# One decoder layer on one core: VectorE in program order at three handovers, a seven-tile start of the mixer, and half of the embedding projection moved

## The chip, the core and the metric

The kernel runs on one core of a Trainium2 chip. Five engines run their own instruction streams: TensorE (PE; its weight loads are shown as PEld), VectorE (DVE), ScalarE (ACT), GpSimd (POOL) and SyncE (SP), which here only starts transfers. The metric is the device time of one execution in microseconds, as the median of several runs.

## What is computed

One step of a decoder layer for 256 prompt columns and 8 sample columns, 264 columns in all:

```python
h = h + 0.5 * rmsnorm(swiglu(rmsnorm(h, ..), w_ffn1_gate, w_ffn1_up, w_ffn1_down), ..)
mix, cb, xb, hs = token_mixer(rmsnorm(h, norm_mix_pre), ...)
h = h + rmsnorm(mix, norm_mix_post)
h = h + 0.5 * rmsnorm(swiglu(rmsnorm(h, ..), w_ffn2_gate, w_ffn2_up, w_ffn2_down), ..)
gate = sigmoid(rmsnorm(h, norm_ple_pre) @ w_ple_gate)
h = h + rmsnorm(gate * (p @ w_ple_proj), norm_ple_post)

# token_mixer(u)
glu_a, glu_b, z, xbc, dt_raw = split(u @ w_in)
v   = silu(layernorm(causal_dwconv31(glu_a * sigmoid(glu_b))))
x, B, C = split(silu(causal_dwconv4(xbc)))       # 3072, 8*128, 8*128
y   = ssd(x, softplus(dt_raw + dt_bias), -exp(a_log), B, C, d_skip, h0)   # 8 groups
yg  = groupwise_rmsnorm(y * silu(z)) * ssm_norm_g
out = concat(v, yg) @ w_out
```

The model width is 2048 (16 tiles of 128 rows, numbered k), the FFN width 5632 (44 tiles). The new states of both convolutions and of the scan are outputs too.

## The kernel before

**Layout and matmuls.** Features lie on the partitions, the 264 columns on the free axis. Each product of a 128x128 weight tile with 128x264 activations is three matmuls (`mm3`, L248 to L252): high part of the weight with the high and the low part of the activation, then the low part of the weight with the high part. So every activation is split in two (`split`, L254: a conversion on ScalarE at L258 or L243, a remainder on VectorE at L216 or L219), and so is every weight.

**Weights.** `PLAN` lists units of up to 16 weight tiles in the order of use. `Weights` (L128 to L165) loads each unit in two halves of up to 8 tiles: a transfer into `wraw` by SyncE, a conversion `whi` on ScalarE (L154), a remainder `wlo` on VectorE (L155). Each has four buffers, two units' worth, and the loading runs two units ahead (`AHEAD`).

**Stages, in order.** FFN 1; *handover 1*; the input projection of the mixer with convolutions, scan and gates between; the output projection; *handover 2*; FFN 2; *handover 3*; the gate projection and the end. At a handover the sum of a norm over all 16 tiles must be complete before the first tile of the next stage can be scaled, and the next stage opens *wide* (`gemm_first`): it runs over k in the outer loop and feeds several output tiles at once, so that it can start with one activation tile. The FFNs and the gate projection open with 7 output tiles (`FIRST_FF`, `FIRST_PG`), the mixer with 4 (dt, B0, C0, x0), in 4 units of 4 k. All other output tiles are computed one by one (`gemm_one`). The accumulators: a pool `acc` of five PSUM banks, a pool `ps` of three. With four tiles open one bank of `acc` is still free; with seven, all five and two of `ps` are taken.

**Handover 1.** `rs` is the scale of the FFN's result, `r` that of the mixer's input; r comes from the same sums by a chain of products (`q2`). The residual is updated for each k by `tt(t, ys[k], rs)` and `tt(H(k), H(k), t)`, and u is `H(k)` times r times a gain. Updates of k above 0 are added on GpSimd, some of the products too. The projection of the per-layer embedding (`pproj`, 96 matmuls in two units `pp`, which depend on nothing in the layer) fills TensorE's time in this gap. The residual is then stored to DRAM (`hsave`).

**The mixer.** `IN_ORDER` lists the output tiles. For each of the 8 groups: B, C, three x, three z, with pairs of GLU tiles (ga, gb) put between at `GLU_IN`. The taps of the long GLU convolution are queued and done a few at a time on VectorE. `do_dt` makes dt, its decays and their sums, with a trip through DRAM to spread them over partitions. `decays` (L696) loads the sums and makes the decay matrices on ScalarE; `ssd` is the scan of a group, with transposes of x on TensorE (L727) and state products (L753). `gate` (L809) multiplies y by Silu(z), squares on ScalarE, adds twice on GpSimd (`SumSq`, tile `run`, L216), sums over partitions by a matmul with ones on TensorE (`total`, L306), and scales. It is called one group late, at x0 of the next group.

**Order.** A list scheduler orders each engine's instructions by its own reckoning of when they are ready, with program order as priority; the engines then run in that order. `high_priority` lifts some. `after` (L243) keeps the activation tables of ScalarE (Silu, Sigmoid, Ln and Exp) in program order, since a change of table is an instruction of its own (L238).

## Time and profile before

| | us |
|---|---|
| median of 3 runs | 2435.34 |
| the runs | 2430.39, 2435.34, 2436.11 |
| profiled execution | 2432.44 |
| its span in the profile | 2430.7 |
| TensorE busy | 2367.7 (97%) |
| VectorE busy | 1569.2 (65%) |
| ScalarE busy | 1181.4 (49%) |
| GpSimd busy | 298.4 (12%) |

The mean granted clock of TensorE is 0.993. A row of the profile's groups names line, engine, operation, output and inputs, then count, busy time, the mean of one in ns, and after a bar the idle time of the engine just before, with what ended it. `PE ps L306 <- POOL run L216` in the list of waits is a matmul of line 306 that waited for a GpSimd operation of line 216 on the tile `run`. A row of a timeline begins with the start time and the duration; rows of the same kind are put together (`x4`), and in brackets stands how long the engine was idle before, and what it waited for. Matmuls are pipelined, so a matmul of 0.28 us in a timeline may be followed by the next after 0.12.

### The profile page before, as it was taken

To read this page: it belongs to the slowest core of one execution; us is meant where nothing else is said; L and a number is where in the kernel's file an instruction comes from. 1 tells how busy PE (TensorE), PEld (TensorE's weight loads), DVE (VectorE), ACT (ScalarE), POOL (GpSimd) and SP (SyncE) were. 2 spreads that over 40 slices of the span, in tenths; PEclk is the share of its full clock that TensorE was granted. 3 is DMA by queue.
4 is the path that set the end of the run, shared out by engine and by line. 5 is a ranking of instruction groups with operands and counts; after the bars stand their busy time and mean duration, and the time that the engine had idled before them with its cause. 6 is when DMAs were issued, how large, how long until landed. Compare 5 with 4: busy or idle time off the path is not lost.

```text
span 2430.7 us, 47409 instructions
## 1 busy us (share of the span) xinstructions
PE 2367.7 (97%) x19448; PEld 2342.7 (96%) x19448; DVE 1569.2 (65%) x2333; ACT 1181.4 (49%) x1771; POOL 298.4 (12%) x295
## 2 busy tenths in 40 slices
PE   8999999999999889999999999999999999999988
PEld 8999999999999889999999999999999999999988
DVE  6554455545557858988798975766545565565585
ACT  6444444433456465665565545544444443344465
POOL 0400000000015212122122010101000000000103
PEclk9999999999999999999999999999999999999999
DMA  7655555555556666666666556476766776676553
GB/s 249 217 183 184 182 183 182 183 183 183 183 169 207 213 180 193 207 216 202 210 216 205 181 181 216 153 238 228 240 213 223 237 236 217 217 236 206 184 191 132
DMA packets 166250, 489.89 MB, mean 202 GB/s; under 512 B 25568, under 2 KB 42640, under 8 KB 166032
## 3 DMA queue, kind: packets, MB, share of 16 engines
q1 hardware_dynamic: 166032, 486.86, 62.0%
q8 instruction: 152, 2.49, 0.4%
q14 instruction: 66, 0.54, 0.1%
HBM read 465.65 MB, written 22.42 MB: 201 GB/s over the span
## 4 chain that ended last, share of the span: by engine, by line
PE 84%; DVE 6%; issue 3%; ACT 3%; DMA 2%; POOL 1%; SPq 0%; ACTq 0%; POOLq 0%; DVEq 0%
PE acc L250 27%; PE acc L251 27%; PE acc L252 27%; DVE wlo L155 2%; DVE y L219 1%; ACT whi L154 1%; PE ps L306 1%; DVE h L216 1%; DMA ab<-d_cs 1%; DMA cbc<-d_bc 1%; DVE ych L794 1%; PE ps L250 0%; ACT tmp L243 0%; DMA d_bc<-rows 0%; PE ps L251 0%
## 5 line engine op out<-in xcount | busy, mean ns | idle before, releaser
L252 PE MATMUL acc<-act,wlo 128*128 128x264 f32 x6224 | 1770.7, 285 | 4.3 <-DVE wlo L155 4.1
L251 PE MATMUL acc<-act,whi 128*128 128x264 f32 x6224 | 1756.6, 283 | 6.3 <-DVE act L216 6.2
L250 PE MATMUL acc<-act,whi 128*128 128x264 f32 x6224 | 1747.7, 283 | 3.4 <-DVE tmp L216 2.1
L155 DVE TENSOR_TENSOR wlo<-wraw,whi 128x1024 fp32r<-128x1024 f32 (+2 forms) x812 | 986.9, 1217 | 597.9 <-ACT whi L154 595.5
L154 ACT CAST whi<-wraw 128x1024 fp32r<-128x1024 f32 (+2 forms) x812 | 829.9, 1026 | 961.9 <-PE acc L251 717.3
L250 PEld LDWEIGHTS acc<-act,whi 128*128 128x128 f32 x6224 | 1175.5, 190 | 6.0 <-issue 2.1
L251 PEld LDWEIGHTS acc<-act,whi 128*128 128x128 f32 x6224 | 1169.2, 188 | 9.9 <-DVE act L216 7.9
L252 PEld LDWEIGHTS acc<-act,wlo 128*128 128x128 f32 x6224 | 1167.9, 188 | 8.3 <-DVE wlo L155 6.4
L216 POOL TENSOR_TENSOR run<-run,tmp 128x264 f32<-128x264 f32 x93 | 87.8, 944 | 962.9 <-ACT tmp L243 961.8
L216 POOL TENSOR_TENSOR s<-s,eap 128x1024 f32<-128x1024 f32 x24 | 48.8, 2035 | 630.4 <-DMA s<-in_hst 630.4
L219 DVE SCALAR_TENSOR_TENSOR y<-v,vec,y 128x251 f32<-128x251 f32 (+23 forms) x240 | 118.1, 512 | 1.2
L219 DVE SCALAR_TENSOR_TENSOR s<-bb,xds,s 128x128 f32<-128x128 f32 x192 | 52.7, 346 | 66.1 <-POOL s L216 66.1
L216 POOL TENSOR_TENSOR h<-h,cbc 128x512 f32<-128x512 f32 x48 | 73.6, 1553 | 166.0 <-DMA cbc<-d_bc 90.9
L258 ACT CAST act<-tmp 128x264 fp32r<-128x264 f32 x120 | 48.7, 410 | 69.9 <-DVE tmp L216 55.2
L216 DVE TENSOR_TENSOR tmp<-acc,rr 128x264 f32<-128x264 f32 x100 | 43.0, 430 | 51.0 <-PE acc L252 50.8
L216 DVE TENSOR_TENSOR tmp<-tmp,acc 128x264 f32<-128x264 f32 x86 | 36.7, 427 | 38.7 <-PE acc L252 38.6
L216 DVE TENSOR_TENSOR act<-tmp,act 128x264 fp32r<-128x264 f32 x120 | 56.1, 471 | 0.3
L243 ACT ACTIVATE tmp<-tmp 128x264 f32<-128x264 f32 x112 | 47.0, 420 | 8.7 <-DVE tmp L216 8.4
L243 ACT ACTIVATE tmp<-y 128x264 f32<-128x264 f32 x67 | 28.0, 425 | 44.1 <-DVE y L216 43.0
L216 DVE TENSOR_TENSOR y<-y,acc 128x264 f32<-128x264 f32 x80 | 34.0, 425 | 24.0 <-PE acc L252 24.0
L794 DVE TENSOR_REDUCE ych<-h 128x4 f32<-128x512 f32 x48 | 32.4, 678 | 17.5 <-POOL h L216 17.5
L250 PE MATMUL ps<-act,whi 128*128 128x264 f32 x96 | 28.4, 304 | 15.4 <-ACT whi L154 8.1
(165 smaller groups left out, 926.1 us busy)
## 6 DMA issues: line engine op xcount, KB each, us to landing
wraw<-in_w SPq DMA_DIRECT2D x756, 512.0 KB, 4.7
h<-in_hst SPq DMA_DIRECT2D x48, 256.0 KB, 3.9
s<-in_hst SPq DMA_DIRECT2D x24, 512.0 KB, 6.5
out_nss<-s SPq DMA_DIRECT2D x24, 512.0 KB, 3.0
wraw<-in_w SPq DMA_DIRECT2D x24, 384.0 KB, 4.1
wraw<-in_w SPq DMA_DIRECT2D x32, 256.0 KB, 3.9
ab<-d_cs SPq DMA_DIRECT2D x16, 384.0 KB, 5.1
cbc<-d_bc SPq DMA_DIRECT2D x8, 512.0 KB, 4.3
```

The source lines that it names most:

```text
L154: nc.scalar.copy(hi, raw)
L155: nc.vector.tensor_tensor(out=lo, in0=raw, in1=hi.bitcast(F32), op=ALU.subtract)
L216: return (eng or nc.vector).tensor_tensor(out=out, in0=in0, in1=in1, op=op)
L219: return nc.vector.scalar_tensor_tensor(out=out, in0=in0, scalar=scalar, in1=in1, op0=op0, op1=op1)
L243: i = nc.scalar.activation(out=out, in_=in_, func=func, bias=bias, scale=scale)
L250: nc.tensor.matmul(acc, hi, x[:, 0, :], start=first, stop=False)
L251: nc.tensor.matmul(acc, hi, x[:, 1, :], start=False, stop=False)
L252: return nc.tensor.matmul(acc, lo, x[:, 0, :], start=False, stop=last).ins
L258: nc.scalar.copy(t[:, 0, :], x)
L306: nc.tensor.matmul(p, ones, s, start=i == 0, stop=i == len(self.parts) - 1)
L794: nc.vector.tensor_reduce(out=ych[:, j, b : b + 4], in_=h0, op=ALU.add, axis=AX.X)
```

## The change

1. **VectorE in program order at the handovers** (`in_order`, `handed`): from the handover until the wide start is issued, VectorE's instructions stand as the program writes them. The program is written so that they interleave: `update_h(0..3)` between the steps of q2, then `make_u(k)` (scale, split, update of k + 4) two per unit of the wide start, through `feed`; `Weights.fill` puts the loads behind them. At handovers 2 and 3 the class `Update` does the same (five steps ahead, then two per unit).
2. **No GpSimd at handover 1**: 15 additions and 7 products go to VectorE.
3. **The mixer opens seven tiles wide** (`FIRST_IN`), in 8 units of 2 k. For group 0 the three z tiles come ahead of C: dt, B0, z0, z1, z2, C0, x0. Then x1, x2, B1 and so on one by one.
4. **`GLU_IN`** has three pairs amid the mixer instead of four; the other five follow at the end.
5. **The second half of the embedding projection** (48 matmuls) moves to handover 3.
6. **Decays**: the sample decay is exponentiated before its trip through DRAM (`ed`) rather than behind it; `load_sums` starts the loads at C, `decays` only computes. For group 0 the scan is put off until B1 has come (`early`).
7. **Gates** in two: `gate_begin` at C of the next group, `gate_end` where `gate` stood, its total no earlier than the last matmul written before it (`traced`).
8. `btm` has two buffers; the stores of the residual come behind the wide start.

What it moves on VectorE at handover 1. Before, from the first product of r's chain (`tmp_9007` is q2, `rr_9000` is rs, `rr_9018` is r, `h_85` holds the residual of the first four k):

```order
492 L216 TENSOR_TENSOR tmp_9007<-ps_9008,rr_9000 128x264
493 L216 TENSOR_TENSOR tmp_9190<-y_2456,rr_9000 128x264
494 L216 TENSOR_TENSOR tmp_9193<-y_2519,rr_9000 128x264
495 L216 TENSOR_TENSOR tmp_9196<-y_2582,rr_9000 128x264
496 L219 SCALAR_TENSOR_TENSOR tmp_9007<-ps_9012,tmp_9007 128x264
497 L216 TENSOR_TENSOR h_85<-h_85,tmp_9190 128x264
498 L216 TENSOR_TENSOR tmp_9007<-tmp_9007,rr_9000 128x264
499 L219 SCALAR_TENSOR_TENSOR tmp_9007<-rr_295,tmp_9007 128x264
500 L155 TENSOR_TENSOR wlo_0_9024<-wraw_0_9022,whi_0_9023 128x1024
501 L155 TENSOR_TENSOR wlo_8_9030<-wraw_8_9028,whi_8_9029 128x1024
502 L219 SCALAR_TENSOR_TENSOR tmp_9199<-h_85,vec,rr_9018 128x264
```

The same place after (q2 is `tmp_9010`, rs `rr_9003`, r `rr_9033`):

```order
494 L226 TENSOR_TENSOR h_85<-h_85,tmp_9015 128x264
495 L229 SCALAR_TENSOR_TENSOR tmp_9010<-ps_9018,tmp_9010 128x264
496 L226 TENSOR_TENSOR tmp_9022<-y_2520,rr_9003 128x264
497 L226 TENSOR_TENSOR h_85<-h_85,tmp_9022 128x264
498 L226 TENSOR_TENSOR tmp_9010<-tmp_9010,rr_9003 128x264
499 L226 TENSOR_TENSOR tmp_9026<-y_2583,rr_9003 128x264
500 L226 TENSOR_TENSOR h_85<-h_85,tmp_9026 128x264
501 L229 SCALAR_TENSOR_TENSOR tmp_9010<-rr_296,tmp_9010 128x264
502 L226 TENSOR_TENSOR tmp_9030<-y_2646,rr_9003 128x264
503 L226 TENSOR_TENSOR h_85<-h_85,tmp_9030 128x264
504 L229 SCALAR_TENSOR_TENSOR tmp_9108<-h_85,vec,rr_9033 128x264
505 L226 TENSOR_TENSOR act_9110<-tmp_9108,act_9110 128x264
```

Before, two remainders of weights stand between the chain and the first product of u, and the sums of the residual are on GpSimd. After, the sums stand between the steps of the chain, and the first u follows with its split directly behind it; the remainders of the second unit come as rows 520 and 521, behind four tiles of u.

VectorE behind the wide start of the mixer. Before (`acc_9341`, `acc_9342` and `acc_9343` are B0, C0 and x0, `h_9584` is dt):

```order
549 L219 SCALAR_TENSOR_TENSOR bc_9627<-acc_9341,vec,bc_9627 128x255
550 L216 TENSOR_TENSOR bc_9627<-bc_9627,shist 128x8
551 L219 SCALAR_TENSOR_TENSOR bc_9627<-acc_9341,vec,bc_9627 128x254
552 L219 SCALAR_TENSOR_TENSOR bc_9627<-acc_9342,vec,bc_9627 128x255
553 L216 TENSOR_TENSOR bc_9627<-bc_9627,shist 128x8
554 L219 SCALAR_TENSOR_TENSOR bc_9627<-acc_9341,vec,bc_9627 128x253
555 L219 SCALAR_TENSOR_TENSOR bc_9627<-acc_9342,vec,bc_9627 128x254
556 L155 TENSOR_TENSOR wlo_8_9532<-wraw_8_9530,whi_8_9531 128x1024
557 L219 SCALAR_TENSOR_TENSOR h_9644<-acc_9343,vec,h_9644 128x255
558 L216 TENSOR_TENSOR h_9644<-h_9644,shist 128x8
559 L219 SCALAR_TENSOR_TENSOR bc_9627<-acc_9342,vec,bc_9627 128x253
560 L577 TENSOR_SCALAR h_9584<-h_9584 48x264
```

After (`ps_9171` is B0, `acc_9175` C0, `h_9698` dt):

```order
578 L229 SCALAR_TENSOR_TENSOR bc_9742<-ps_9171,vec,bc_9742 128x255
579 L226 TENSOR_TENSOR bc_9742<-bc_9742,shist 128x8
580 L614 TENSOR_SCALAR h_9698<-h_9698 48x264
581 L229 SCALAR_TENSOR_TENSOR bc_9742<-acc_9175,vec,bc_9742 128x255
582 L226 TENSOR_TENSOR bc_9742<-bc_9742,shist 128x8
583 L229 SCALAR_TENSOR_TENSOR bc_9742<-ps_9171,vec,bc_9742 128x254
584 L615 RECIPROCAL h_9698<-h_9698 48x264
585 L229 SCALAR_TENSOR_TENSOR bc_9742<-acc_9175,vec,bc_9742 128x254
586 L159 TENSOR_TENSOR wlo_8_9689<-wraw_8_9687,whi_8_9688 128x1024
587 L229 SCALAR_TENSOR_TENSOR bc_9742<-ps_9171,vec,bc_9742 128x253
588 L229 SCALAR_TENSOR_TENSOR h_9698<-tmp_9703,h_9698 48x264
589 L229 SCALAR_TENSOR_TENSOR bc_9742<-acc_9175,vec,bc_9742 128x253
```

The third step on C0, the row that frees the bank in which x1 is accumulated after the change, now has the reciprocal of the dt chain ahead of it; before, the dt chain came later and x1 had a bank of its own.

TensorE at the total of group 0's gate. Before (`run_10316` is the sum of squares, the accumulator is that of one z tile):

```order
7309 L252 MATMUL acc_10827<-act_9257,wlo_0_10578 128x264
7310 L250 MATMUL acc_10827<-act_9265,whi_8_10583 128x264
7311 L251 MATMUL acc_10827<-act_9265,whi_8_10583 128x264
7312 L306 MATMUL ps_10325<-run_10316,ones 128x264
7313 L727 MATMUL ps_10647<-ident,h_10307 128x128
```

After (`run_10475` is that sum):

```order
7260 L262 MATMUL acc_10761<-act_9361,whi_8_10495 128x264
7261 L263 MATMUL acc_10761<-act_9361,whi_8_10495 128x264
7262 L264 MATMUL acc_10761<-act_9361,wlo_8_10496 128x264
7263 L319 MATMUL ps_10559<-run_10475,ones 128x264
7264 L768 MATMUL ps_10580<-ident,h_10246 128x128 x2
```

In both the total stands amid the same z tile, at its ninth activation tile, one matmul later than before; VectorE's product of the gate stands in both between the remainders of the same two units of weights.

The diff, cut to its core:

```diff
-FIRST_FF, FIRST_PG = 7, 7
-GLU_IN = (1, 2, 4, 6)
+FIRST_FF, FIRST_IN, FIRST_PG = 7, 7, 7
+GLU_IN = (1, 3, 5)
...
-    for q in range(2):
-        plan.append(("pp", [0, 1], list(range(8 * q, 8 * q + 8))))
-    first = [m for _, m in IN_ORDER[:4]]
-    for q in range(4):
-        plan.append(("in", k16[4 * q : 4 * q + 4], first))
+    plan.append(("pp", [0, 1], list(range(8))))
+    first = [m for _, m in IN_ORDER[:FIRST_IN]]
+    for q in range(8):
+        plan.append(("in", k16[2 * q : 2 * q + 2], first))
...
     ffn(2)
+    plan.append(("pp", [0, 1], list(range(8, 16))))
...
-    for k in range(KD + 2):
+    def update_h(k):
+        t = tmp()
+        tt(t, ys[k], rs, ALU.mult)
+        tt(H(k), H(k), t, ALU.add)
+
+    def make_u(k):
         if k < KD:
             t = tmp()
-            tt(t, ys[k], rs, ALU.mult, nc.gpsimd if k % 2 and k > 2 else nc.vector)
-            tt(H(k), H(k), t, ALU.add, nc.gpsimd if k else nc.vector)
-        if k >= 2:
-            t = tmp()
-            stt(t, H(k - 2), V("mix_pre", k - 2), r, ALU.mult, ALU.mult)
+            stt(t, H(k), V("mix_pre", k), r, ALU.mult, ALU.mult)
             us.append(split(t))
+        if k + 4 < KD:
+            update_h(k + 4)
+
+    q2 = tmp()
+    tt(q2, yy.total(), rs, ALU.mult)
+    update_h(0)
+    stt(q2, hy.total(), 2.0, q2, ALU.mult, ALU.add)
+    update_h(1)
...
+    project(0, pacts)
+    for k in range(4):
+        make_u(k)
+    ws.fill()
...
-        nc.sync.dma_start(d_dt[1], dta[:, NP_:])
+        ed = mp.tile([P, NS], F32, name="ed")
+        act(ed[:NH], dta[:, NP_:], AF.Exp)
+        nc.sync.dma_start(d_dt[1], ed[:NH])
...
-        act(eap, eap, AF.Exp)
...
-            b = mp.tile([P, P], F32, tag="btm", bufs=1, name=nm("btm"))
+            b = mp.tile([P, P], F32, tag="btm", bufs=2, name=nm("btm"))
...
-    def gate(g, y, zs):
+    def gate_begin(g, y, zs):
+
         tt(y, y, zs, ALU.mult)
         sq = SumSq(3, direct=0)
         for j in range(3):
             sq.add(y[:, j, :])
+        return g, y, sq
+
+    def gate_end(g, y, sq):
+
         t = tmp()
-        rsqrt(t, sq.total(), eps1, 1.0 / 384)
+        rsqrt(t, sq.total(traced[0]), eps1, 1.0 / 384)
...
-    first = gemm_first(us, k16, 4)
+    first = gemm_first(
+        us, k16, 8, FIRST_IN, feed=lambda: [make_u(len(us)) for _ in range(2) if len(us) < KD]
+    )
+    handed.close()
...
+    class Update:
...
+        def step(self, n=2):
+            for _ in range(n):
+                k, self.k = self.k, self.k + 1
+                if k < KD:
+                    residual(k, ys[k], *self.args)
+                if 1 <= k <= KD:
+                    self.xs.append(split(H(k - 1), V(self.pre, k - 1)))
+                if 3 <= k < KD + 3:
+                    self.sq.add(H(k - 3))
...
+    pacts = load_p()
+    in_order()
     rs = ffn_scale(ysq, eq)
-    xs, sq = update_input(rs, "ffn2_post", "ple_pre")
+    project(1, pacts)
+    u3 = Update(rs, "ffn2_post", "ple_pre")
+    ws.fill()
```

148 lines of the change are left out of this document (93 added, 55 removed).

## The prediction

> **What bounds the kernel now.** I read the page first: which engine is busy, and what the chain that ended last is made of.
>
> ```profile
> PE 2367.7 (97%) x19448; PEld 2342.7 (96%) x19448; DVE 1569.2 (65%) x2333; ACT 1181.4 (49%) x1771; POOL 298.4 (12%) x295
> PE 84%; DVE 6%; issue 3%; ACT 3%; DMA 2%; POOL 1%; SPq 0%; ACTq 0%; POOLq 0%; DVEq 0%
> ```
>
> TensorE bounds it, and the matmuls stay the same in number. A gain can come only from stretches in which TensorE waits or runs at a lower clock. The view of TensorE's waits lists the first kind (engine, tile and line that waited, what was waited for: us, times, longest):
>
> ```profile
> PE ps L306 <- POOL run L216: 12.0, 9, 2.6
> PE ps L250 <- ACT act L243: 7.4, 2, 3.7
> PE ps L727 <- ACT h L243: 7.3, 2, 4.9
> PE acc L251 <- DVE act L216: 6.2, 7, 1.6
> PE acc L252 <- DVE wlo L155: 4.1, 8, 0.9
> PE ps L753 <- ACT btm L736: 1.1, 1, 1.1
> ```
>
> Then windows of one stage each (start:end, length, then busy time and count of matmuls and weight loads, VectorE, ScalarE, GpSimd, granted clock, DMA share, GB/s):
>
> ```profile
> 100.00:300.00 200.00, 200.00 (x1669) 200.00 (x1668) 96.72 (x97) 83.40 (x105) 9.55 (x19) 1.00 0.58 183
> 780.00:835.00 55.00, 47.85 (x362) 45.71 (x361) 50.53 (x78) 29.72 (x60) 23.60 (x24) 0.97 0.69 230
> 855.00:880.00 25.00, 17.67 (x120) 17.14 (x119) 10.74 (x18) 17.81 (x36) 0.00 (x0) 0.86 0.53 153
> 1540.00:1560.00 20.00, 14.98 (x105) 14.14 (x104) 16.56 (x39) 13.34 (x28) 0.75 (x1) 0.83 0.23 78
> 2310.00:2330.00 20.00, 15.08 (x102) 14.25 (x102) 16.72 (x38) 12.87 (x27) 0.83 (x1) 0.83 0.28 93
> ```
>
> The first row, deep in FFN 1, gives the full rate: 200/1669 = 0.1198 us a matmul. A stage's length less its count at that rate is what it loses: handover 1 (780 to 835) 55 − 362 × 0.1198 = 11.6 us; the opening of the mixer (855 to 880) 25 − 14.4 = 10.6; handover 2 20 − 12.6 = 7.4; handover 3 20 − 12.2 = 7.8. With the gates' 12.0 that is 49 us, what this change aims at. Transposes are counted as matmuls, so each may be some tenths off.
>
> Part of the loss is clock. TensorE alone, in windows of 3.41 us (busy and count, clock, DMA share, GB/s):
>
> ```profile
> 787.80:791.22 3.42, 1.70 (x12) 1.00 0.74 215
> 791.22:794.63 3.41, 3.39 (x15) 0.50 0.99 379
> 920.93:924.34 3.41, 0.93 (x6) 1.00 0.59 193
> 924.34:927.75 3.41, 3.41 (x18) 0.50 0.79 276
> 1542.16:1545.57 3.41, 1.34 (x6) 1.00 0.33 96
> 1545.57:1548.98 3.41, 0.46 (x2) 0.50 0.47 175
> 1548.98:1552.39 3.41, 3.41 (x17) 0.50 0.00 0
> ```
>
> A window that is half idle or more is followed by one at half clock, which holds 15 to 18 matmuls where 28.5 fit: some 1.4 us lost, 1.7 where 15. I take 1.7.
>
> By the Trainium skill (TensorE: Matmul & The Clock Gate, the HAM clock gate) the half rate follows at least one idle window of about 3.4 us. Here windows 0.93 to 1.70 us busy were enough. By the page's rule the sum below would be about 1.7 us less, since of the opening's two slow windows only the one behind its longest wait would stay.
>
> **Handover 1.** The durations come from the uncontended rows at handover 2 and in the mixer, the conversion of u and the last weight rows from the grouped lines, the rest from timelines:
>
> ```profile
> 1543.42 0.95 DVE L155 TENSOR_TENSOR wlo<-wraw,whi 128x768 fp32r<-128x768 f32 x1
> 1545.87 1.71 DVE L219 SCALAR_TENSOR_TENSOR tmp<-y,vec,rr 128x264 f32<-128x264 f32 x4 [1.50 <-ACT rr L243]
> 1547.49 1.46 DVE L216 TENSOR_TENSOR h<-h,tmp 128x264 f32<-128x264 f32 x4
> ...
> 1545.33 0.42 ACT L243 ACTIVATE rr<-rr 128x264 f32<-128x264 f32 x1
> 1547.95 0.52 ACT L243 ACTIVATE act<-h,vec 128x264 fp32r<-128x264 f32 x1 [2.20 <-DVE h L216]
> ...
> L258 ACT CAST act<-tmp 128x264 fp32r<-128x264 f32 x16 | 6.6, 412 | 14.7 <-DVE tmp L219 14.7
> ...
> L155 DVE TENSOR_TENSOR wlo<-wraw,whi 128x1024 fp32r<-128x1024 f32 x11 | 13.4, 1216 | 11.4 <-ACT whi L154 11.4
> ...
> 781.10 0.43 DVE L216 TENSOR_TENSOR tmp<-ps,rr 128x264 f32<-128x264 f32 x1 [2.16 <-PE ps L306]
> ...
> 788.15 1.38 DVE L219 SCALAR_TENSOR_TENSOR tmp<-h,vec,rr 128x264 f32<-128x264 f32 x2
> ...
> 789.63 0.76 PE L250 MATMUL acc<-act,whi 128*128 128x264 f32 x4 [0.89 <-ACT act L258]
> ```
>
> VectorE takes 1.71/4 = 0.43 for a scaled product and 1.46/4 = 0.37 for a sum; an engine hands over in 1545.87 − (1545.33 + 0.42) = 0.12. Beside GpSimd the same product took 1.38/2 = 0.69, and the 22 GpSimd operations go, so I take the short ones. Now the chain of r is ten operations in program order from 781.10, about 0.4 each, to 785.1; Ln and Exp (0.43 each) to 786.0; u0's product, handover and conversion 0.43 + 0.12 + 0.41 + 0.12: TensorE starts at 787.1, before at 789.6. But half of the 96 projection matmuls (48 × 0.1198 = 5.8 us) has gone from this gap: by the order 13 are left behind the totals, which are there at 781.1, instead of 61, so TensorE runs dry at 782.6 instead of 789.63 − 0.89 = 788.7. From there VectorE sets the pace. A tile of u costs it 0.43 + 0.12 + 0.41 + 0.12 (it stands still for the conversion, since its next row needs that) + 3 × 0.37 = 2.19; a unit is two tiles and 1.22 + 0.95 of weight remainders: 6.55 us, against 42 × 0.1198 = 5.03 on TensorE. The remainders of unit 1 stand behind four tiles (786.0 + 8.8 + 1.2 = 796.0), those of units 2 to 5 follow at 6.55 each (822.2), units 6 and 7 without updates at 5.1 (832.4), and 28 more matmuls end the wide start at W = 835.8. From 780 that is 22 + 336 matmuls in 55.8 us, a loss of 12.9 against 11.6: **+1.3** (−2 to +4; half a window more or less, and 0.1 us a tile).
>
> **The opening of the mixer.** The seven tiles hold all five accumulators and two of three other banks; before, x1 had a fifth one free. The rows that it must now wait for:
>
> ```profile
> L219 DVE SCALAR_TENSOR_TENSOR h<-acc,vec,h 128x254 f32<-128x254 f32 (+2 forms) x5 | 2.3, 469 | 0.0
> ...
> L581 DVE RECIPROCAL h<-h 48x264 f32<-48x264 f32 x1 | 1.8, 1786 | 0.0
> ...
> L154 ACT CAST whi<-wraw 128x1024 fp32r<-128x1024 f32 x13 | 13.5, 1044 | 13.2 <-PE acc L251 13.2
> L238 ACT ACT_TABLE_LOAD x3 | 3.8, 1283 | 0.0
> ...
> L243 ACT ACTIVATE h<-h 128x264 f32<-128x264 f32 x3 | 1.1, 412 | 0.0
> ```
>
> x1 takes C0's bank, free after C0's third convolution step. VectorE reaches the weights of x1 at W − 2.5 (behind unit 7's second half, 832.4 + 0.95), two remainders take it to W, and then come two more remainders (2.4), six steps (2.8), the reciprocal (1.8) and some 1.3 (an estimate) of small rows: W + 8.3. x1 then runs 5.8, to W + 14.1. x2 takes z0's bank, and z0's Silu stands on ScalarE behind the second conversion of weights 148, whose buffer x1 frees as it ends: 14.1 + 1.04, a table load of 1.28, cd and two Silus, 1.3 with handovers: a wait of 3.8 (an estimate). The transposes of x2 wait some 2.0 for its own Silu, as before's second one did. With two half-clock windows (3.4) that is 17.5. What goes is before's 10.6: there the transposes waited for Silu behind decays and a DMA round trip, which now have three more tiles to finish in. **+6.9** (0, if the banks come free early, to +9).
>
> The table load has a row; by the Trainium skill (ScalarE: Activation LUTs, What ACT_TABLE_LOAD costs) a switch is about 2.66 us with its drain. In the rows here the next operation follows after 1.28, so 1.4 more for x2 is not in the sum.
>
> **The gates.** A gate's product, squares and two GpSimd sums end in a total on TensorE:
>
> ```profile
> 923.41 0.71 PE L306 MATMUL ps<-run,ones 128*128 128x264 f32 x2 [2.57 <-POOL run L216]
> ```
>
> The split starts the product at C of the next group and lets the total stand behind x at the earliest. In the new order, though, the total stands as far behind VectorE's product as it did: for group 0 behind 27 matmuls of tile 156 instead of 26, for group 1 34 instead of 35, over all eight on average one matmul more (0.12 us). 8 × 0.12 = 1, of which I take **−0.7** (−12 to +2).
>
> **Handover 2.** Before, four products (1.71) come ahead of the first sum; now product 0 and sum 0 are first, so the first conversion starts after 0.80 instead of 1545.87 to 1547.95 = 2.08. TensorE starts 1.2 us earlier, but in a window that the table above shows at half clock whatever happens: about 0.9 with the chance of one slow window less. **−0.9** (−2.6 to +1, where VectorE's 5.4 us a unit against 5.03 shows).
>
> **Handover 3.** The other 48 projection matmuls, 5.8 us, stand in this gap:
>
> ```profile
> 2314.71 0.71 PE L306 MATMUL ps<-tmp,ones 128*128 128x264 f32 x2 [1.29 <-ACT tmp L243]
> ...
> 2319.06 0.81 PE L250 MATMUL ps<-act,whi 128*128 128x264 f32 x2 [3.63 <-ACT act L243]
> ```
>
> Of them 31 come ahead of the total, which itself waits for them, and 17 behind, 2.0 us. ScalarE's order has the copies of the projection and two weight conversions (2 × 1.04 at most) ahead of the first activation. I count 2.9 idle and one slow window: 4.6 instead of 7.8, **−3.2** (−5 to −1).
>
> **Small edits.** Two btm buffers: the 1.1 us wait goes, **−1.1** (−1.1 to 0). One pair of GLU tiles fewer amid the mixer: its taps delay remainders, 4.1 us over four pairs, **−1.0** (−2 to +1). SyncE now waits for one Exp (0.4) before the store of the decays, behind the dt chain, and has the residual's four stores and the loads of the decay sums in other places; what queues behind them are weight transfers, and two units of weights (2 × 5.8 us) are loaded ahead. Priced at nothing; if that cover fails, at a window of half clock (1.7).
>
> **Sum**: 1.3 + 6.9 − 0.7 − 0.9 − 3.2 − 1.1 − 1.0 = +1.3 us. The profiled execution took 2432.44 (span 2430.7), 2.9 under the median of 2435.34; so 2433.7 beside it, 2436.6 beside the median. I say 2436. A measurement of this kernel can tell about 0.3% (7.3 us) from nothing.
>
> **Rivals.**
> - *The totals wait no more* (0.15). For: the split is built so. Against: the distances in the order. The 12.0 us and a slow window of 1.7 go, less my 0.7: 13 less, 2423.
> - *The banks come free early* (0.13): x1 starts as C0's bank is drained before the reciprocal, the opening loses no more than before. 6.9 less: 2429.
> - *VectorE stays slow in the wide start* (0.15), the other side. Mechanism: its operations keep the long durations of before, 0.69 instead of 0.43 for the product, whatever slows them besides GpSimd (weights arriving, ScalarE's conversions). Two tiles with five operations each at about 0.2 us more are 2 us a unit; over six units 12: 2448. It decides from 0.5 us a mean 264-column operation on.
> - *The later handovers gain nothing* (0.10): the projection's copies and conversions on ScalarE hold the first activation as long as the waits did. 4.1 more: 2440.
>
> **Numbers.** The forecast has 0.47. Its own terms (±3, ±4, ±2) put it at 2429 to 2442. Faster by over 0.3% (under 2428): the first rival 0.15, half of the second, some 0.06 of the forecast: 0.28. Slower (over 2442.6): the third 0.15, 0.03 of the fourth, 0.06 of the forecast: 0.24. Same: 0.48. For 8 in 10 the range goes from 2422, which takes in the first rival, to 2447, which leaves out half of the third.
>
> **What would show it.** Right: TensorE idle some 4.5 us ahead of the wide start, then short waits for remainders of unit 1 to 5; one gap of about 8 us ahead of x1, its releaser a convolution on VectorE; waits of the totals for GpSimd still 8 to 12 us; the gap of handover 3 under 3 us. Wrong: the opening free of gaps over 3 us, or the totals' row under 5 us (faster), or a product of u at 0.6 us and more (slower).

## The result

| | us |
|---|---|
| the kernel before, median of 4 runs | 2432.86 (2430.28 to 2436.11) |
| the changed kernel, median of 4 runs | 2457.75 (2457.16 to 2458.73) |
| ratio of the times | 1.0107 (95%: 1.0093 to 1.0120) |
| its profiled execution, and the span of it | 2457.87, 2456.2 |

The change made the kernel 1.07% slower, some 25 us, outside the range of the prediction. The page of the changed kernel, in the lines that were shown of before, with the list by line below them:

```profile
PE 2376.7 (97%) x19444; PEld 2352.6 (96%) x19444; DVE 1575.5 (64%) x2359; ACT 1186.5 (48%) x1777; POOL 279.3 (11%) x273
PE 82%; DVE 6%; DMA 5%; ACT 3%; issue 2%; POOL 1%; SPq 0%; ACTq 0%; DVEq 0%; POOLq 0%
PE acc L262 27%; PE acc L263 26%; PE acc L264 26%; DMA wraw<-in_w 3%; DVE wlo L159 2%; ACT whi L158 1%; POOL run L226 1%; DVE y L229 1%; DMA d_bc<-rows 1%; DVE h L226 1%; PE ps L319 1%; DVE h L229 1%; DVE ych L835 1%; ACT tmp L253 0%; POOL h L226 0%
```

The list by line of the kernel before:

```profile
PE acc L250 27%; PE acc L251 27%; PE acc L252 27%; DVE wlo L155 2%; DVE y L219 1%; ACT whi L154 1%; PE ps L306 1%; DVE h L216 1%; DMA ab<-d_cs 1%; DMA cbc<-d_bc 1%; DVE ych L794 1%; PE ps L250 0%; ACT tmp L243 0%; DMA d_bc<-rows 0%; PE ps L251 0%
```

Transfers hold 5% of the chain that ended last where they held 2%, and 3% of it are the weights (`wraw<-in_w`), which before the change were not in that list at all. TensorE's waits after the change:

```profile
PE ps L319 <- POOL run L226: 14.9, 9, 3.4
PE ps L264 <- DVE wlo L159: 10.9, 6, 3.1
PE ps L262 <- ACT whi L158: 8.8, 2, 8.5
PE acc L262 <- DVE bc L229: 8.5, 1, 8.5
PE acc L262 <- ACT tmp L253: 7.0, 1, 7.0
PE ps L262 <- ACT act L253: 4.8, 2, 2.6
PE ps L262 <- ACT act L271: 4.0, 1, 4.0
PE acc L262 <- ACT h L253: 3.1, 1, 3.1
PE acc L264 <- DVE wlo L159: 2.7, 3, 1.9
```

The 8.5 us for `bc` are x1's, the 3.1 for `h` x2's, both as forecast. New are 10.9 us for remainders of weights (`wlo`) in the wide start, and 7.0 us in one piece for `tmp`.

To see where the time went I cut every trace into the same stretches, each from the start of one matmul to that of another that follows the same work, and took from its length 0.1198 us for each matmul in it, as in the prediction. Handover 1 ends as x1's wait begins; the opening ends in the GLU pair of group 1; handover 3 reaches 64 matmuls into the single tiles of the gate projection. What is left is what the stretch loses, in us:

| kernel | handover 1 | opening | mixer | handover 2 | handover 3 | span |
|---|---|---|---|---|---|---|
| before | 13.2 | 11.8 | 28.2 | 9.2 | 10.1 | 2430.7 |
| changed | 23.4 | 18.2 | 34.0 | 9.1 | 12.7 | 2456.2 |
| difference | +10.2 | +6.4 | +5.8 | −0.1 | +2.6 | +25.5 |

The rest of the kernel makes up the last half microsecond. In handover 3 the first part loses 3.1 instead of 8.6, but the stretch behind its wide start 9.6 instead of 1.5.

Windows of the changed kernel (columns as in the prediction): a stretch of FFN 1, handover 1, the core of the mixer, and the end of the gate projection's wide start; then the mixer of before.

```profile
100.00:300.00 200.00, 200.00 (x1669) 200.00 (x1668) 96.28 (x98) 83.99 (x105) 12.43 (x26) 1.00 0.57 183
780.00:845.50 65.50, 50.60 (x361) 48.74 (x359) 43.93 (x85) 25.03 (x44) 0.50 (x2) 0.92 0.51 167
930.00:1350.00 420.00, 406.07 (x3296) 392.85 (x3296) 350.94 (x588) 240.35 (x431) 90.58 (x63) 0.98 0.65 205
2370.00:2420.00 50.00, 42.96 (x335) 42.44 (x334) 32.30 (x48) 33.35 (x59) 10.82 (x10) 0.90 0.64 220
```

```profile
930.00:1350.00 420.00, 405.49 (x3330) 391.36 (x3329) 362.13 (x620) 242.35 (x441) 85.63 (x66) 1.00 0.65 205
```

The full rate is unchanged. At handover 1 GpSimd is all but idle as intended (busy 0.50 of 65.50 us), but VectorE, which was to set the pace, is busy only 43.93 of 65.50, where it was busy 50.53 of 55 before: it waits too. In the mixer the clock of 0.98 stands for four windows at half rate, 13.7 us in all (two from 993.0 us on, one each at 1119.3 and 1177.3); before there were none in that window. Over the whole span TensorE was granted half the clock for 67.2 us, where it was 31.8 before (mean clock 0.986 and 0.993). If TensorE had work all that time, the 35.4 us more cost 17.7 (an estimate, and an upper bound, since some of it falls in waits). So up to some two thirds of the 25.5 us are clock that was lost, mostly right behind waits; the stretches hold both.

### The profile page after: what moved, and what is told of

It is laid out like the page before. It is cut to its first block, busy times and chain, and to the rows that moved or that the text cites. A ratio compares the mean times of both kernels' runs of the same rounds, so it can differ in the third digit from the quotient of the medians.

```text
span 2456.2 us, 47408 instructions
## 1 busy us (share of the span) xinstructions
PE 2376.7 (97%) x19444; PEld 2352.6 (96%) x19444; DVE 1575.5 (64%) x2359; ACT 1186.5 (48%) x1777; POOL 279.3 (11%) x273
## 4 chain that ended last, share of the span: by engine, by line
PE 82%; DVE 6%; DMA 5%; ACT 3%; issue 2%; POOL 1%; SPq 0%; ACTq 0%; DVEq 0%; POOLq 0%
PE acc L262 27%; PE acc L263 26%; PE acc L264 26%; DMA wraw<-in_w 3%; DVE wlo L159 2%; ACT whi L158 1%; POOL run L226 1%; DVE y L229 1%; DMA d_bc<-rows 1%; DVE h L226 1%; PE ps L319 1%; DVE h L229 1%; DVE ych L835 1%; ACT tmp L253 0%; POOL h L226 0%
## 5 line engine op out<-in xcount | busy, mean ns | idle before, releaser
L264 PE MATMUL acc<-act,wlo 128*128 128x264 f32 x6192 | 1750.3, 286 | 2.8 <-DVE wlo L159 2.7
L229 DVE SCALAR_TENSOR_TENSOR y<-v,vec,y 128x227 f32<-128x227 f32 (+27 forms) x240 | 116.3, 510 | 1.1
L262 PE MATMUL ps<-act,whi 128*128 128x264 f32 x128 | 36.0, 301 | 17.5 <-ACT whi L158 8.8
L226 DVE TENSOR_TENSOR y<-y,acc 128x264 f32<-128x264 f32 x80 | 34.0, 425 | 24.1 <-PE acc L264 24.0
L264 PE MATMUL ps<-act,wlo 128*128 128x264 f32 x128 | 35.1, 301 | 10.9 <-DVE wlo L159 10.9
```

Of the source, the lines that this page charges most:

```text
L226: return (eng or nc.vector).tensor_tensor(out=out, in0=in0, in1=in1, op=op)
L229: return nc.vector.scalar_tensor_tensor(out=out, in0=in0, scalar=scalar, in1=in1, op0=op0, op1=op1)
L262: nc.tensor.matmul(acc, hi, x[:, 0, :], start=first, stop=False)
L264: traced[0] = nc.tensor.matmul(acc, lo, x[:, 0, :], start=False, stop=last).ins
```

## The experiments

Most of these kernels ran once. The runs of the kernel before lie between 2423.34 and 2436.11 us, five of one changed version (three_bank) between 2434.47 and 2443.32, so a single run tells differences of the whole from about 9 us up. Smaller ones are read from the stretches of its trace, and these vary too: where an edit leaves the mixer's order on TensorE as it was (changed, act_units, fill_first, ho3_free), the mixer loses 32.5 to 35.6 us. A small edit can also move rows elsewhere, since the scheduler plans anew. Five kernels (act_order, bank and the three at the end) have one more wait in handover 2, 3.0 us for an activation that ScalarE converts; why, no run shows. The stretches of all of them:

| kernel | handover 1 | opening | mixer | handover 2 | handover 3 | span |
|---|---|---|---|---|---|---|
| act_order | 18.1 | 18.2 | 29.2 | 14.0 | 12.3 | 2450.2 |
| act_units | 13.9 | 18.4 | 35.6 | 9.0 | 11.3 | 2448.2 |
| fill_first | 21.1 | 18.0 | 34.2 | 9.2 | 12.7 | 2454.0 |
| pp_back | 21.6 | 16.9 | 31.3 | 8.7 | 9.9 | 2446.4 |
| half_only | 17.3 | 12.3 | 27.4 | 10.2 | 8.6 | 2434.4 |
| ho3_free | 23.6 | 17.6 | 32.5 | 8.9 | 8.3 | 2448.7 |
| dt_late | 24.5 | 16.9 | 38.3 | 8.0 | 11.9 | 2457.7 |
| open4 | 23.2 | 7.8 | 37.9 | 7.9 | 15.1 | 2449.8 |
| bank | 22.2 | 17.9 | 30.9 | 14.0 | 12.0 | 2454.9 |
| gate_z | 23.8 | 18.7 | 31.0 | 8.9 | 12.9 | 2453.2 |
| glu4 | 24.3 | 17.8 | 21.5 | 9.0 | 12.7 | 2443.9 |
| before_glu3 | 13.4 | 8.7 | 35.0 | 9.4 | 10.1 | 2434.7 |
| before_glu7 | 13.2 | 10.2 | 27.3 | 9.5 | 10.3 | 2429.3 |
| mixer_only | 13.2 | 11.9 | 26.3 | 8.8 | 9.8 | 2428.4 |
| three | 12.0 | 17.0 | 24.1 | 10.3 | 13.3 | 2435.1 |
| three_free | 13.9 | 20.2 | 16.4 | 12.5 | 9.9 | 2431.4 |
| three_bank | 13.9 | 19.8 | 26.3 | 13.7 | 8.5 | 2441.5 |

### Handover 1: who keeps VectorE waiting

In the changed kernel a unit of the wide start takes 803.85 − 795.51 = 8.3 us, not 6.55. One unit on VectorE, then on ScalarE, then SyncE's transfers:

```profile
795.51 2.08 DVE L159 TENSOR_TENSOR wlo<-wraw,whi 128x1024 fp32r<-128x1024 f32 x2
...
799.64 0.49 DVE L229 SCALAR_TENSOR_TENSOR tmp<-h,vec,rr 128x264 f32<-128x264 f32 x1
802.69 0.43 DVE L226 TENSOR_TENSOR act<-tmp,act 128x264 fp32r<-128x264 f32 x1 [2.55 <-ACT act L271]
803.04 0.43 DVE L226 TENSOR_TENSOR tmp<-y,rr 128x264 f32<-128x264 f32 x1
803.50 0.43 DVE L226 TENSOR_TENSOR h<-h,tmp 128x264 f32<-128x264 f32 x1
803.85 2.09 DVE L159 TENSOR_TENSOR wlo<-wraw,whi 128x1024 fp32r<-128x1024 f32 x2
```

```profile
798.03 0.41 ACT L271 CAST act<-tmp 128x264 fp32r<-128x264 f32 x1 [2.81 <-DVE tmp L229]
801.29 1.05 ACT L158 CAST whi<-wraw 128x1024 fp32r<-128x1024 f32 x1 [2.85 <-DMA wraw<-in_w]
802.25 0.41 ACT L271 CAST act<-tmp 128x264 fp32r<-128x264 f32 x1
```

```profile
796.75 9.57 SPq L157 DMA_DIRECT2D wraw<-in_w  x4
```

VectorE's scaled tile is there at 800.1 and needs ScalarE's conversion, which comes at 802.25: ahead of it in ScalarE's queue stands the conversion of a later unit's weights, and that waits 2.85 us for a transfer which started at 796.75. It could not start sooner: its buffer is one that the remainders of 795.51 were the last to read. So the remainders that VectorE's program order puts late delay a transfer, and ScalarE's order, which is the scheduler's, hands the delay back to VectorE. Over the wide start ScalarE waits 16.5 us for weights; before, none.

**act_order.** ScalarE too in program order from handover 1 on.

```diff
-    def in_order():
-        handed.enter_context(tc.manual_schedule(engines={mybir.EngineType.DVE}))
+    def in_order(*more):
+        handed.enter_context(tc.manual_schedule(engines={mybir.EngineType.DVE, *more}))
...
-    in_order()
+    in_order(mybir.EngineType.Activation)
     rs = ffn_scale(ysq, eq)
```

> Changed kernel, but ScalarE too stands in program order at handover 1, so that the conversion of a later unit's weights comes behind the two conversions of u instead of between them. Theory (the weights' conversion waits for a transfer that starts late, and the conversion of u, and so VectorE, waits behind it): VectorE's idle time of some 2.5 us per unit of the wide start goes, the units take about 6.7 us instead of 8.3, the stretch from 780 us to x1 loses 13 to 15 us instead of 22.6, the whole 2448 to 2450 us instead of 2457.75. Rival (VectorE's own work, slowed by transfers, sets the pace): the stretch loses 20 us or more, the whole stays within 2 us of the changed kernel.

Measured: 2451.89 us (the kernel before, run beside it: 2427.84). The stretch loses 5.3 us less, between the two forecasts. Units take 6.26 us, but the copies of the projection now stand behind r on ScalarE and open a gap of 5.3 us ahead of the wide start.

**act_units.** The same without that gap:

```diff
     project(0, pacts)
+    handed.enter_context(tc.manual_schedule(engines={mybir.EngineType.Activation}))
     for k in range(4):
```

> Changed kernel, ScalarE in program order only from the first tile of u to the end of the wide start of the mixer; the copies of the projection stay ahead of r, unlike in the earlier run with ScalarE in order, which had a gap of 5.3 us there. Theory (ScalarE's queue passes the late transfers on to u): a unit takes 6.2 to 6.7 us instead of 8.3, the stretch from 780 us to x1 loses 15 to 18 us instead of 22.6; what is then left above the 13 us of the kernel before is VectorE's own pace. Rival: 20 us or more, the earlier run having gained by something else.

Measured: 2449.93 us (before: 2432.93). ScalarE in it, over the same time:

```profile
799.16 0.41 ACT L271 CAST act<-tmp 128x264 fp32r<-128x264 f32 x1 [1.71 <-DVE tmp L229]
799.48 1.78 ACT L158 CAST whi<-wraw 128x1024 fp32r<-128x1024 f32 x2
803.29 0.41 ACT L271 CAST act<-tmp 128x264 fp32r<-128x264 f32 x1 [2.04 <-DVE tmp L229]
```

The conversion of the weights no longer stands ahead of u's. The stretch loses 13.9 us, 0.7 more than before the change: 9.5 of the 10.2 us were ScalarE's queue. The wide start ends at 835.5 us, where the changed kernel's ends at 845.5.

**fill_first.** The other end of the ring: the projection asks for the next weights, as before the change.

```diff
-        w = ws.next(fill=False)
+        w = ws.next()
```

> Changed kernel with one line undone: the projection of the embedding asks for the next weights as before the change (next without fill=False), so that at handovers 1 and 3 the remainders of the second unit stand ahead of the new steps on VectorE and every later transfer starts a unit earlier. Theory (the weights run one unit short, each transfer waits for a remainder that VectorE's program order has put late, and ScalarE's queue passes that wait on): ScalarE's waits for transfers in the wide starts fall from 16.5 and 13.2 us to under 4 each; the stretch of handover 1 to x1 is 7 to 11 us shorter, the wait of 7.0 us behind the wide start of handover 3 falls under 3.5; the whole 11 to 16 us shorter than the changed kernel. Rival (VectorE's own work sets the pace): under 3 us shorter at handover 1.

Measured: 2455.78 us (before: 2430.48). At handover 1 only 2.3 us less, and ScalarE still waits 12.3 us for weights: one unit more in hand is used up after three units. At handover 3 ScalarE's waits fall from 13.2 to 2.3 us, but the wait behind the wide start only from 7.0 to 4.5, and the restart comes 2.1 us later. The theory was right about the order on ScalarE, wrong that this line is its cause.

### Handover 3: the wait behind its wide start

The end of the wide start in the changed kernel, ScalarE and VectorE:

```profile
2378.11 0.48 ACT L253 ACTIVATE rr<-ps,eps 128x264 f32<-128x264 f32 x1
2378.62 0.42 ACT L253 ACTIVATE rr<-rr 128x264 f32<-128x264 f32 x1
2379.06 1.28 ACT L248 ACT_TABLE_LOAD   x1
2380.77 1.04 ACT L158 CAST whi<-wraw 128x1024 fp32r<-128x1024 f32 x1 [0.42 <-DVE tmp L226]
2383.83 1.04 ACT L158 CAST whi<-wraw 128x1024 fp32r<-128x1024 f32 x1 [2.02 <-DMA wraw<-in_w]
2384.78 0.73 ACT L253 ACTIVATE tmp<-tmp 128x264 f32<-128x264 f32 x2
```

```profile
2377.34 0.43 DVE L226 TENSOR_TENSOR run<-run,tmp 128x264 f32<-128x264 f32 x1
...
2384.91 1.23 DVE L159 TENSOR_TENSOR wlo<-wraw,whi 128x1024 fp32r<-128x1024 f32 x1 [1.84 <-ACT whi L158]
2386.05 0.77 DVE L226 TENSOR_TENSOR e<-e,tmp 128x264 f32<-128x264 f32 x2
2386.74 0.43 DVE L226 TENSOR_TENSOR tmp<-acc,rr 128x264 f32<-128x264 f32 x1
```

The sum of squares ends at 2377.77 and r at 2379.04, 1.2 us before the wide start ends (2380.27). Then the Sigmoid stands behind two conversions of weights, one of which waits 2.02 us for a transfer, and VectorE's product that frees a bank stands behind it all: it ends at 2387.17, and TensorE goes on at 2387.31.

**pp_back.** Both halves of the projection at handover 1.

```diff
-    plan.append(("pp", [0, 1], list(range(8))))
+    for q in range(2):
+        plan.append(("pp", [0, 1], list(range(8 * q, 8 * q + 8))))
...
     project(0, pacts)
+    project(1, pacts)
```

> Changed kernel, but both halves of the embedding projection stay at handover 1. Theory (the wait of 7.0 us behind the wide start of the gate projection comes from weights that arrive late and a norm that VectorE's program order finishes late, not from the projection): that wait stays at 5 us or more, handover 3 loses 4 to 6 us more, the gap of 4.0 us at handover 1 goes, but VectorE's pace keeps the rest: 0 to 6 us longer than the changed kernel. Rival (the projection's stores and the embedding's loads on SyncE hold up the weights there): the wait falls under 2 us, the whole is 2 to 8 us shorter.

Measured: 2448.08 us (before: 2427.84). The wait falls to 3.2 us, between the two, and the whole is 9.7 us shorter than the changed kernel, where the theory had it up to 6 longer. Handover 3 as a whole loses 2.8 us less than with the half projection in it, and handover 1 1.8 less.

**half_only.** That half alone, on the kernel before.

```diff
     ffn(2)
+    plan.append(("pp", [0, 1], list(range(8, 16))))
...
+    pacts = load_p()
     rs = ffn_scale(ysq, eq)
+    project(1, pacts)
```

> The kernel before with one part of the change alone: half of the embedding projection moved to handover 3. Theory: handover 3 loses 3.5 to 5.5 us less, with no wait over 2.5 us behind its wide start, since the projection there fills the weights ahead; handover 1, where 48 matmuls less cover the chain, loses 0 to 4 us more because the scaled tiles set its pace anyway; the whole is 0 to 5 us shorter than the kernel before. Rival (the projection itself delays the gate projection's weights and first tiles): 3 us longer or more, with the wait of 5 us or more behind the wide start of handover 3.

Measured: 2436.09 us (before: 2430.48). Handover 3 loses 1.5 us less with no long wait behind it (1.2), handover 1 4.1 us more. By the spans it costs 3.7 us, less than runs of one kernel differ by; the gain expected does not show, and the rival's wait does not either.

**ho3_free.** No program order on VectorE at handover 3:

```diff
     pacts = load_p()
-    in_order()
     rs = ffn_scale(ysq, eq)
     project(1, pacts)
```

> Changed kernel without VectorE's program order at handover 3 alone; the projection's second half, the steps and the weights' filling there stay as changed. Theory (the wait of 7.0 us behind the wide start of the gate projection comes from VectorE's program order, which finishes the norm and the remainders late): the wait falls under 3 us, the stretch from 2335 us on loses 4 to 7 us less, at the price of 0 to 2 us at the restart. Rival (the projection's missing fill alone makes the weights late): the wait stays at 5 us or more.

Measured: 2450.45 us (before: 2428.38). TensorE's waits from 2335 to 2400 us in it:

```profile
PE ps L263 <- DVE act L229: 2.4, 1, 2.4
PE ps L262 <- ACT act L253: 2.1, 1, 2.1
PE acc L262 <- DVE tmp L226: 1.2, 1, 1.2
```

The 7.0 us are gone, 2.4 come at the restart, handover 3 loses 8.3 instead of 12.7. So the wait needs VectorE's program order; the projection in that gap makes it longer, as pp_back showed.

### The opening of the mixer

**dt_late.** The chain of dt behind the convolutions of B0, C0 and x0.

```diff
         if kind == "dt":
-            do_dt(acc)
+            dt_acc = acc
...
                 else:
+                    do_dt(dt_acc)
                     load_sums(g)
```

> Changed kernel, but the chain of dt is written behind the convolutions of B0, C0 and x0 instead of ahead of them. Theory (x1 waits because the dt chain with its reciprocal stands ahead of the convolution steps that free C0's bank, and x2 because the Silu of z0 stands behind that chain on ScalarE): the wait of 8.5 us ahead of x1 falls to 4 to 6, that of 3.1 us ahead of x2 to under 1, the opening loses 9 to 13 us instead of 17.8, the whole is 5 to 9 us shorter. Rival (VectorE is behind in any order, and the late dt chain brings back the wait of the transposes): the opening loses 16 us or more, the whole stays within 2 us.

Measured: 2459.53 us (before: 2427.84). x1 still waits 6.9 us, x2 no more, and up to the first scan the opening loses some 8 us less. Then a wait of 4.3 us for the scan's state products, with a window at half clock, takes 7 of them back: the opening gains 1.3 us in all, and the mixer loses 4.3 more.

**bank.** One of the five accumulators left free for x1 (`held=4` in gemm_first).

```diff
-        accs = [ps_tile([P, T]) if m < nm - 5 else acc_tile() for m in range(nm)]
+        accs = [ps_tile([P, T]) if m < nm - held else acc_tile() for m in range(nm)]
```

> Changed kernel, with the third tile of the mixer's wide start accumulated in the other pool of banks, so that one of the five accumulators is free for x1, as it was before the change. Theory (x1's wait of 8.5 us is for a bank): that wait goes, x2 waits 2 to 5 us for the next bank, the opening loses 5 to 9 us less, the whole is 4 to 9 us shorter than the changed kernel. Rival (VectorE and the dt chain hold the opening whatever the banks): the wait moves to x2 and the transposes, under 2 us shorter.

Measured: 2456.56 us (before: 2428.28). The waits from 845 to 890 us:

```profile
PE acc L262 <- DVE bc L229: 4.1, 1, 4.1
PE ps L768 <- ACT h L253: 4.0, 1, 4.0
PE acc L262 <- ACT h L253: 3.8, 1, 3.8
```

x1 starts at once, and x2, B1 and the transposes wait 11.9 us together, as x1 and x2 did (11.6). The bank is where the wait shows, not what it costs: the rival was right.

**open4.** The opening as before: four tiles wide, z behind x, the first scan at x2.

```diff
-FIRST_FF, FIRST_IN, FIRST_PG = 7, 7, 7
+FIRST_FF, FIRST_IN, FIRST_PG = 7, 4, 7
...
-    for q in range(8):
-        plan.append(("in", k16[2 * q : 2 * q + 2], first))
+    for q in range(4):
+        plan.append(("in", k16[4 * q : 4 * q + 4], first))
```

> Changed kernel, but the mixer opens as before the change: four tiles wide in four units, z behind x, the first scan at x2; program order, GpSimd's part, gates and all else as changed. Theory (with five accumulators taken and the dt chain ahead, x1 and x2 wait): the waits of 8.5 and 3.1 us go, those of the transposes come back at 5 to 8 us; the stretch to x1 gains nothing, since sixteen tiles of u at 2.2 us are on VectorE alone with less to do beside them (0 to 4 us lost); the whole is 2 to 8 us shorter. Rival (the seven-tile start is a gain at handover 1 that outweighs its opening): 3 us longer or more.

Measured: 2451.58 us (before: 2430.48). The opening loses 7.8 us instead of 18.2, the transposes do not wait, the first state products wait 4.0; handover 1 is unchanged; the whole is 6 us shorter, with the mixer and handover 3 3.9 and 2.4 us worse. What covers the dt chain is single tiles behind the wide start. With four tiles wide, x1, x2 and the three z are such tiles; with seven, the z are already spent, in a stretch in which TensorE waits for VectorE anyway. That reading fits open4 and bank; no run shows it by itself.

### The mixer: gates and GLU pairs

**gate_z.** The totals behind the third z tile of the next group.

```diff
             if j == 0:
-                finish_gate()
                 if g:
...
             act(zs[:, j, :], acc, AF.Silu)
+            if j == 2 and g > 1:
+                finish_gate()
```

> Changed kernel, but the second half of a gate is written behind the third z tile of the next group instead of its first x tile (groups 1 to 6), so that the totals cannot stand earlier than there. Theory (the scheduler puts a total where its own reckoning has the GpSimd sums ready, and on the chip they are 1.3 to 3.4 us later; the longer waits also bring half-clock windows): waits of the totals for GpSimd fall from 14.9 us to under 6, three or four of the five half-clock windows of the mixer go, the whole is 12 to 18 us shorter, 2440 to 2446 us. Rival (the sums move with the totals, or the later gates hold buffers): waits of 10 us or more, the whole under 5 us shorter.

Measured: 2454.93 us (before: 2427.84). TensorE's waits from 885 to 1400 us, first of the changed kernel, then of this one:

```profile
PE ps L319 <- POOL run L226: 14.7, 8, 3.4
PE acc L264 <- DVE wlo L159: 2.7, 3, 1.9
PE acc L262 <- ACT v L253: 1.5, 1, 1.5
```

```profile
PE acc L264 <- DVE wlo L159: 12.7, 10, 2.0
PE ps L768 <- ACT h L253: 4.3, 4, 2.9
PE ps L319 <- POOL run L226: 3.0, 2, 2.0
```

The totals wait 3.0 instead of 14.7, as the theory had it, and the remainders of weights 12.7 instead of 2.7: the mixer gains 3 us, not 12 to 18. The 3 us are no more than the mixer varies by. VectorE is busy 351 of the 420 us from 930 on in the changed kernel; I take it to be behind either way, so that the total had only been the first to show it, but that is argued from where the waits went.

**glu4.** Four GLU pairs amid the mixer again.

```diff
-GLU_IN = (1, 3, 5)
+GLU_IN = (1, 2, 4, 6)
```

> Changed kernel with four GLU pairs amid the mixer, as before the change. Theory (the pairs are tiles without convolutions, in which VectorE and GpSimd catch up; with one fewer the gates' sums come later): the stretch from 890 us to the output projection loses 4 to 6 us less, the totals wait 11 to 12.5 us instead of 14.9. Rival (the mixer's longer waits come from the split gates and the late first scan): within 1.5 us of the changed kernel.

Measured: 2445.6 us (before: 2430.48), the largest gain of any single edit. Its waits from 885 to 1400 us:

```profile
PE ps L319 <- POOL run L226: 7.2, 7, 1.3
PE acc L264 <- DVE wlo L159: 4.7, 3, 3.7
```

The mixer loses 21.5 us instead of 34.0. The direction was expected, the size was more than twice what I had written: with shorter waits the half-clock windows went too, all four between 930 and 1350 us.

**before_glu3** and **before_glu7**: the kernel before with `GLU_IN = (1, 3, 5)`, and with `GLU_IN = (1, 2, 3, 4, 5, 6, 7)`.

> The kernel before with three GLU pairs amid the mixer instead of four, as the changed kernel has, and nothing else. Theory (a pair is 11.5 us of matmuls without a convolution or scan, in which VectorE and GpSimd catch up): the mixer loses 8 to 12 us more, by longer waits of the totals for GpSimd and for remainders of weights, the whole is 2438 to 2443 us where the kernel before takes 2428 to 2436. Rival (only with the split gates does the missing pair cost anything): within 3 us of the kernel before.

> The kernel before with seven GLU pairs amid the mixer, one after x of each group from the second on, instead of four. Theory (the pairs are breathing space): the waits of the totals for GpSimd fall from 12.0 to under 5 us, one or two half-clock windows go, the whole is 4 to 10 us shorter than the kernel before. Rival (four pairs already give enough, and the taps of the long convolution come at the wrong time): 2 us shorter at most, or longer.

Measured: 2436.39 and 2431.09 us (before: 2432.93). Three pairs cost the mixer 6.8 us, less than the 8 to 12 expected, of which the opening gives back 3.1; the totals wait 15.7 us. Seven pairs gain 0.9 us in the mixer, and the totals wait 13.8 us, no less than the 12.0 with four. So a missing pair hurts, more pairs do not help, and a pair is no simple breathing space.

**mixer_only.** The small edits of the mixer alone on the kernel before: split gates, `load_sums` at C, `ed`, two btm buffers.

```diff
-            b = mp.tile([P, P], F32, tag="btm", bufs=1, name=nm("btm"))
+            b = mp.tile([P, P], F32, tag="btm", bufs=2, name=nm("btm"))
...
             do_conv(acc, m - MT_X, bct[:, 1, :])
+            begin_gate()
+            if m > MT_CM:
+                load_sums(m - MT_CM)
```

> The kernel before with only the small edits of the mixer: split gates, loads of the decay sums at C, the sample decay ahead of its trip, two btm buffers; four GLU pairs, no program order, opening and projection as before. Theory (these edits are the good part of the change, hidden by the missing GLU pair): the opening and the mixer lose 6 to 12 us less, the whole is 5 to 12 us shorter than the kernel before. Rival (with totals placed as before, they change nothing): within 3 us.

Measured: 2430.06 us (before: 2432.93). Opening and mixer lose 1.8 us less: the rival, no change that a single run can tell.

### Do the parts add up?

**three**: `GLU_IN` of glu4, pp_back and the line of act_units together. **three_free**: glu4, act_units and ho3_free together. **three_bank**: three_free and bank.

> Changed kernel with three things mended together: four GLU pairs amid the mixer, both halves of the projection at handover 1, ScalarE in program order through the wide start of the mixer. Theory (three separate faults, which alone gave spans 12.3, 9.8 and 8.0 us shorter; the second and third overlap at handover 1 by some 2): span 24 to 29 us shorter than the changed kernel, 2427 to 2432 us, so about equal to the kernel before. Rival (what one frees is lost to the next wait, as when the gates were put off): 15 us shorter at most.

> Changed kernel with three things mended together: four GLU pairs amid the mixer, ScalarE in program order through the wide start of the mixer, and VectorE not in program order at handover 3, with the projection's second half left there. Theory: as the sum of its parts, 12 for the pairs, 8 for ScalarE's order and 4 to 7 for handover 3, it is 22 to 28 us shorter than the changed kernel, span 2428 to 2434 us. Rival (gains do not add): 15 us shorter at most.

> The three mended things of the last run with handover 3 out of program order, and the free bank for x1 besides. Theory: the opening, the one stretch in which that kernel still loses more than the kernel before (20.2 against 11.8 us), gives back 5 to 9 us; the whole is 2426 to 2432 us where the run without the bank took 2435, and from 0.1% faster than the kernel before to 0.2% slower. Rival: 2433 us or more.

| kernel | runs | median us | beside the kernel before | ratio (95%) |
|---|---|---|---|---|
| three | 4 | 2437.06 | 2428.38 | 1.0041 (1.0026 to 1.0056) |
| three_free | 10 | 2435.19 | 2428.38 | 1.0027 (1.0017 to 1.0037) |
| three_bank | 5 | 2440.76 | 2428.28 | 1.0036 (1.0022 to 1.0049) |

The span of three_free is 24.8 us shorter than that of the changed kernel; its three parts alone gave 12.3, 8.0 and 7.5, together 27.8. They add up within 3 us, inside what was expected. But that is one trace of each: by the ratios beside runs of the kernel before, 1.0107 falls to 1.0027, so that some three quarters of the loss are given back. Nor does each stretch return to what it was: in three_free the opening loses 8.4 us and handover 2 3.3 more than before the change, and the mixer 11.8 less. With the same order of TensorE in the mixer, glu4 lost 21.5 there; it has a wait of 3.7 us for a remainder at the start, at 918.5, that three_free does not have. With three the sum was 30.1 and the gain 21.1, less than expected: the wait behind handover 3 is 4.0 us, after 3.2 in pp_back. For three_bank the rival was right: the free bank gave the opening 0.4 us, and the scheduler's order in the mixer moved, which lost 26.3 us instead of 16.4 in a run that was the slowest of five. No version beats the kernel before.

## Why the prediction was wrong

**Handover 1** (+1.3 forecast, +10.2 measured). The step that failed is "The remainders of unit 1 stand behind four tiles ..., those of units 2 to 5 follow at 6.55 each". That was worked out from VectorE's own rows and the handover to an idle ScalarE. I had read VectorE's order and had not asked what stands ahead of u's conversion in ScalarE's, nor from when that waits. With that cause taken out (act_units), the wide start ends at 835.5 us, where I had 835.8, and the stretch loses 0.7 us more than before, inside the range of the term. A term that I put at nothing failed with it: two units of weights loaded ahead were to cover what queues late, and ScalarE waited 16.5 us for transfers there, since buffers now come free behind the late remainders. The restart was right: 787.58 against 787.1. The rival of slow VectorE operations was wrong: a product took 0.49, a sum 0.43.

**Opening** (+6.9 forecast, +6.4 measured). Right in place and size: x1 waits 8.5 (8.3 forecast), x2 3.1 (3.8). The sum is in part luck: the transposes, at 2.0 in it, wait 0.2, and behind the two waits TensorE runs 11.1 us at half clock, which cost 5.5 where I had 3.4:

```profile
854.03:859.83 5.80, 5.80 (x24) 0.50 0.26 86
868.21:873.49 5.28, 5.28 (x24) 0.50 0.56 185
```

Not right was its cause as I put it, a bank that the reciprocal's place keeps taken: with another bank the stretch loses as much within 0.3 us, with a later chain within 1.3. The chain does hold x1 and x2 (dt_late takes 1.6 and 3.1 us off their waits), but the first scan needs it as badly. The sentence that the decays "now have three more tiles to finish in" has it the wrong way round, as open4 suggests.

**Gates and mixer** (−0.7 − 1.1 − 1.0 forecast, +5.8 measured). That the totals would still wait was right (14.7 after 11.8), and so was that the btm wait goes. The step that failed is the one on the small edits, "One pair of GLU tiles fewer amid the mixer ... −1.0": I had priced what a pair costs, its taps on VectorE, and not what it gives. It is the change's costliest line: putting the pair back gains 12.5 us in the mixer. That it gives 11.5 us of matmuls during which no total or scan is due is argued; no run shows that this is why. With the changed kernel, ten have this mixer code or nearly so and three pairs, and lose 29 to 38 us there; the four with four pairs lose 16 to 26. Why the same line costs the kernel before 6.8 and there is nothing to be had from seven pairs stays open; the totals' places in the scheduler's order, which change with the number of pairs, may be part of it.

**Handover 2** (−0.9 forecast, −0.1 measured). TensorE's second wait fell from 3.74 to 2.65 us much as forecast, but TensorE then runs 5.2 us at half clock, where it was 3.9 before, and most of the time is given back.

**Handover 3** (−3.2 forecast, +2.6 measured). The gap itself gave 5.5 us, more than forecast. The step that failed is that I stopped there, and put what comes behind the wide start at nothing. TensorE waits 7.0 us there: by VectorE's program order the sums for r, the remainders of late weights and the products that free the banks stand one behind the other at its end. In ho3_free, without that order, handover 3 loses 1.8 us less than before the change.

**The size of the whole.** Three of the causes, taken out together, give back 24.8 of 25.5 us by the spans of single traces, and some three quarters by the ratios. The opening is not among them: that the z tiles' early place costs it is argued from open4. The faster rival (totals that wait no more) shows in gate_z what it would have been worth: 3 us, not 13, as waits for VectorE's remainders came in its place.

## What to carry to other kernels

Fixing one engine's order fixes what it releases, too: follow each row that was put late to the buffer that it frees, the transfer that waits for the buffer, and the queue in which that transfer's reader stands ahead of something urgent. Before a tile is moved out of a stretch, ask what it covered there, not only what it costs. And a wait that goes is worth only the distance to the next wait of the same engine: gate_z and bank removed 12 and 8 us of waits and gained 3 and 0.3 in their stretches.

## What was not expected of the hardware

A transfer of 512 KB of weights was usable 4.5 us after its issue (796.75 to 801.29; the median of all 750 such transfers is 4.7), nearly a whole unit of the wide start (5.03 us of matmuls), so a transfer that is released a unit late is late. And the clock added to the mixer's waits: 2.9 us more of waits for totals came with 13.7 us at half rate in the window from 930 to 1350 us, where the kernel before had none. Over the whole kernel 35.4 us more at half rate came with a loss of 25.5.
